# Expert slots by pairs in a two-layer mixture-of-experts kernel

## The chip, the cores and the metric

The kernel runs on one core of one Trainium2 chip. The time is the device time of one execution in microseconds (us); lower is better. TensorE (PE) multiplies, VectorE (DVE) and ScalarE (ACT) work on vectors, GpSimd (POOL) issues the indirect gathers and scatters, and SyncE (SP) issues the large transfers from HBM. Each engine runs its own program in order and waits on semaphores; branches are executed by every engine for itself.

## What is computed

Two blocks run one after the other. The first has two layers of attention and a mixture of experts, the second a mixer of three branches and a feed-forward part. The change is in the mixture of experts of the first block, which sees 512 tokens in layer 0 and 256 in layer 1:

```python
def hier_moe(h, w_group, b_group, w_router, b_router, w1, w3, w2):
    ...
    _, g_idx = lax.top_k(g_logits, 1)                      # one of 4 groups
    ...
    top_v, top_i = lax.top_k(e_in, TOP_K_IN_GROUP)         # two of its 8 experts
    weights = g_w * jax.nn.softmax(top_v, -1)
    experts = g_idx * EXPERTS_PER_GROUP + top_i
    ...
    def expert_block(a):
        xb, e = a
        return (jax.nn.silu(xb @ w1[e]) * (xb @ w3[e])) @ w2[e]
    ...
    return jnp.zeros((t, d), h.dtype).at[tok_s].add(w_s[:, None].astype(h.dtype) * yb[dest])
```

There are 32 experts a layer with 6 MB of weights each (w1 and w3 1024x512, w2 512x1024, all float32). How many rows an expert gets is known only on the chip.

## The kernel before

`route_tokens` works out on the chip which expert gets which rows. It counts the rows of every expert (`size`), ranks the experts by size, and gives each a column of a table of slots (`uc`), from which `gtab` (which rows to gather), the scatter tables and `meta`/`meta2` (expert number and count by place) are made. This is a chain of short DVE operations with a few small matmuls among them; the first gather (on POOL) waits for `gtab`, and PE for the gathered rows.

`experts` then has a fixed list of turns. The first two turns take the two largest experts ("any"). After them `round_(i)` stands nested, one for each i, with a place for a large expert (more than 64 rows; only as long as there can be one, `most[0]`, 15 in layer 0 and 7 in layer 1) and a place for a small one. Large experts fill their places from the front by size, small ones from the back, so the smallest come first. Each place is a branch on the count: `n > 0` runs the turn, the Else only transposes the rows for the next turn. The program stops at the first round in which both places are empty (L1185).

A turn (`turn`) loads six pieces of weights (`expert_weights`, L977 to L980; `wpiece` issues each on SP at L143, 1 MB, into a ring of 6 tiles plus 10 in layer 0 and 12 in layer 1), gathers the rows of the turn two turns ahead (`ahead`), and computes in blocks of up to 128 rows. By the number of rows a block is a quarter (up to 32, L1018 and L1035), a half (up to 64, L1046 and L1061) or full (L1071 and L1086). Each is a first group of matmuls over pieces 0 to 3 and a second over pieces 4 and 5. Between the two the rows of the next turn are transposed (`rows_T`, L995 on PE, L997 on ACT). ACT copies the result (`ys`, L1038, L1064, L1089), which is the end of a turn below, and POOL scatters it. A large expert with more than 128 rows goes on with `rest`; the branch around the rest (L1166) carries a hint for PE that it is likely taken.

SP runs ahead of PE as far as the ring lets it. Each transfer waits on the lane (semaphore) of the earlier transfer that used it, and on PE for the tile that it overwrites. In the Else of a place SP has no transfer to issue but raises the same semaphores by hand (L1180), each after the earlier transfer on that lane has landed, so that later waits count alike on both ways.

With this kernel's inputs layer 0 has 15 used experts and layer 1 has 14.

Of the kernel before, what the change touches and what calls it, by code (L numbers as in the profile page):

```python
# [19 lines left out]
P = 128  # L20
# [6 lines left out]
NE = 32  # L27
# [70 lines left out]
class Builder:  # L98
# [665 lines left out]
    def route_tokens(self, l, nt, gp, mp, rp):  # L764
# [11 lines left out]
        units = mt([NE, 2 * NE], "units")  # L776
        nc.vector.tensor_copy(units[:, 0:NE], self.iota[0:NE, 0:NE])
        nc.vector.tensor_scalar(units[:, NE:], self.iota[0:NE, 0:NE], -1.0, float(NE - 1), ALU.mult, ALU.add)
# [76 lines left out]
        rn = mt([NE, 2], "rn")  # L855
        nc.vector.tensor_reduce(rn[:, 0:1], before, AX.X, ALU.add)
        used = mt([NE, NE], "used")
        nc.vector.tensor_scalar(used, srow, 0.0, None, ALU.is_gt)
        nc.vector.tensor_reduce(rn[:, 1:2], used, AX.X, ALU.add)
# [5 lines left out]
        uh = mt([NE, 2 * NE], "uh")  # L865
        nc.vector.tensor_scalar(uh, units, uc, None, ALU.is_equal)
# [7 lines left out]
        nc.tensor.matmul(mb[0:NE, 0:2 * NE], lhsT=eix, rhs=uh, start=True, stop=True)  # L874
        mb2 = self.bankB()
        nc.tensor.matmul(mb2[0:NE, 0:2 * NE], lhsT=cnt, rhs=uh, start=True, stop=True)

        meta = keep([1, 4 * NE], "meta", I32)
        nc.vector.tensor_copy(meta[:, 0:2 * NE], mb[0:1, 0:2 * NE])
        nc.vector.tensor_copy(meta[:, 2 * NE:4 * NE], mb2[0:1, 0:2 * NE])  # L880
# [38 lines left out]
        for out, parts in ((tb, self.iota[:, 0:P]), (sb, self.cst[:, C_IOTAM:C_IOTAM + P]),  # L919
# [13 lines left out]
            if out is tb:  # L933
# [6 lines left out]
                meta2 = keep([1, 7 * NE], "meta2", I32)  # L940
                for i in range(2):
                    c = slice(2 * NE * i, 2 * NE * i + 2 * NE)
                    nc.vector.scalar_tensor_tensor(meta2[:, c], gtab[0:1, 0:2 * NE], 0.0, meta[:, c], ALU.mult, ALU.add)
# [3 lines left out]
                nc.vector.tensor_tensor(meta2[:, 6 * NE:7 * NE - 2], meta2[:, 4 * NE + 2:5 * NE],  # L947
                                        meta2[:, 5 * NE:6 * NE - 2], ALU.add)
# [33 lines left out]
    def experts(self, l, nt, mp, first, meta, meta2, gtab, stabs, XG, XE, ybuf):  # L982
# [121 lines left out]
        turns = [("any", 0, 0), ("any", 1, 1)]  # L1104
        for i in range(NE - 2):
            turns += [("large", i, 2 + i)] * (i < most[0]) + [("small", i, NE - 1 - i)]

        def ahead(k):
            if k + AHEAD < len(turns):
                kind, _, slot = turns[k + AHEAD]  # L1110
                gather(slot * nt, XG[k % AHEAD], 64 if kind == "small" else P)

        def turn(k, n, W):

            kind, i, slot = turns[k]
            x = XT[k % 2]
            groups = nt if kind == "any" else 1 + sum(i < m for m in most[1:nt]) if kind == "large" else 1

            def block(g, size, b=lambda: None):
# [4 lines left out]
                two(slot * nt + g, W, ht)  # L1124
# [625 lines left out]
```

## Time and profile before

| | us |
|---|---|
| median of 3 runs | 2325.39 (2325.28 to 2330.71) |
| profiled execution | 2326.15, its span 2324.3 |
| PE busy | 1948.4 (84%) |
| DVE, ACT, POOL busy | 1002.8 (43%), 739.9 (32%), 272.6 (12%) |
| HBM read | 455.65 MB, 202 GB/s over the span |

The span is the time from the first instruction to the last in one profiled execution. The granted clock of PE was 0.912 of full speed over it. The largest transfers are the expert weights, 174 pieces of 1 MB. The two mixture-of-experts stretches lie at about 415 to 800 us and 1055 to 1337 us.

To read the rows below: a row of a timeline gives the start, the duration, the engine, the line, the operation with what it writes and reads, the count of merged instructions, and in brackets how long the engine sat idle before it and what ended that. A row of a source line gives the number of instructions and their shortest, median and longest duration in ns, with the first and last start.

### The profile page before, as it was taken

How to read it: one execution, taken by the hardware profiler on the slowest of the kernel's cores; microseconds unless marked ns; L12 is line 12 of the kernel's file. 1: busy time of each engine (PE TensorE's matmuls, PEld its weight loads, DVE VectorE, ACT ScalarE, POOL GpSimd, SP SyncE). 2: the span in 40 equal slices, each digit the busy share in tenths (PEclk: the TensorE clock that was granted, in tenths of full speed). 3: DMA queues.
4: the chain of work that ended last, by engine and by line, in shares of the span. 5: the costliest groups of instructions: out<-in, count | busy, mean ns of one | idle time of the engine just before them, and what ended most of it. 6: DMA issues, size and time to landing. Idle time of an engine off the chain costs nothing. (4 is left out here: it accounts for less than half of the span.)

```text
span 2324.3 us, 27711 instructions
## 1 busy us (share of the span) xinstructions
PE 1948.4 (84%) x10138; PEld 1348.4 (58%) x10138; DVE 1002.8 (43%) x1956; ACT 739.9 (32%) x1322; POOL 272.6 (12%) x214
## 2 busy tenths in 40 slices
PE   6999796778876489977865549999899899998997
PEld 3656575334433167753432237777688677776885
DVE  3346655300000174561000056656654567566554
ACT  2233431100111154411111045444444355434442
POOL 0002301101111052120111102000200020002000
PEclk9999797789997789978987769999999999998998
DMA  9974115354767762156668764344455434454550
GB/s 396 375 280 155 65 37 217 130 209 187 317 255 296 276 239 70 42 205 273 242 253 340 307 241 169 129 145 168 163 186 185 152 129 147 143 181 150 184 181 29
DMA packets 75147, 456.01 MB, mean 196 GB/s; under 512 B 13544, under 2 KB 14092, under 8 KB 24496
## 3 DMA queue, kind: packets, MB, share of 16 engines
q1 hardware_dynamic: 61632, 430.99, 49.5%
q0 software_dynamic: 9664, 14.79, 1.8%
q10 hardware_dynamic: 3632, 7.37, 0.9%
q8 instruction: 129, 2.11, 0.4%
q14 instruction: 90, 0.74, 0.1%
HBM read 455.65 MB, written 13.30 MB: 202 GB/s over the span
## 5 line engine op out<-in xcount | busy, mean ns | idle before, releaser
L167 DVE TENSOR_TENSOR whl<-w,whl 128x1024 fp32r<-128x1024 f32 x312 | 397.1, 1287 | 234.9 <-ACT whl L166 224.2
L166 ACT ACTIVATE whl<-w 128x1024 fp32r<-128x1024 f32 x332 | 344.4, 1057 | 260.5 <-PE bankA L180 208.0
L178 PE MATMUL bankA<-whl,x2h 128*128 128x512 f32 (+1 forms) x864 | 345.3, 400 | 9.6 <-ACT x2h L238 7.2
L180 PE MATMUL bankA<-whl,x2l 128*128 128x512 f32 (+1 forms) x864 | 345.0, 400 | 5.8 <-DVE x2l L239 5.8
L179 PE MATMUL bankA<-whl,x2h 128*128 128x512 f32 (+1 forms) x864 | 342.0, 397 | 0.0
L178 PEld LDWEIGHTS bankA<-whl,x2h 128*128 128x128 f32 x864 | 168.4, 195 | 43.8 <-ACT x2h L238 8.2
L180 PEld LDWEIGHTS bankA<-whl,x2l 128*128 128x128 f32 x864 | 167.4, 194 | 40.6 <-DVE x2l L239 7.2
L179 PEld LDWEIGHTS bankA<-whl,x2h 128*128 128x128 f32 x864 | 167.9, 194 | 35.0 <-issue 2.0
L1071 PE MATMUL bankA<-w,xt 128*128 128x512 f32 x320 | 153.1, 641 | 17.2 <-issue 14.7
L1018 PE MATMUL bankA<-w,xt 128*32 128x256 f32 x1216 | 97.3, 463 | 55.5 <-DMA w<-in_wmoe 32.2
L178 PE MATMUL bankA<-whl,xh 128*128 128x512 f32 (+1 forms) x336 | 132.5, 395 | 5.4 <-ACT xh L238 5.4
L179 PE MATMUL bankA<-whl,xh 128*128 128x512 f32 (+1 forms) x336 | 129.4, 385 | 5.1 <-DVE whl L167 5.1
L180 PE MATMUL bankA<-whl,xl 128*128 128x512 f32 (+1 forms) x336 | 127.8, 384 | 0.1
L414 ACT ACTIVATE p<-bankS,sm 128x256 f32<-128x256 f32 (+2 forms) x160 | 85.7, 537 | 117.6 <-DVE sm L405 59.4
L1071 PEld LDWEIGHTS bankA<-w,xt 128*128 128x128 f32 x320 | 65.0, 206 | 99.7 <-issue 98.3
L213 POOL TENSOR_TENSOR sm<-sm,mhalf 128x1 f32<-128x1 f32 (+3 forms) x32 | 32.2, 1006 | 690.9 <-DVE sm L211 679.3
L1018 PEld LDWEIGHTS bankA<-w,xt 128*32 128x32 f32 x1216 | 47.7, 131 | 102.7 <-issue 44.7
L1022 DVE TENSOR_TENSOR s<-s,bankA 64x256 f32<-64x256 f32 x19 | 8.0, 423 | 221.9 <-ACT s L1021 221.9
L1000 POOL DMA_INDIRECT ybuf<-ys,stab x34 | 34.6, 1019 | 523.6 <-ACT ys L1038 147.1
L1075 DVE TENSOR_TENSOR s<-s,bankA 128x512 f32<-128x512 f32 x10 | 6.9, 688 | 195.2 <-PE bankA L1071 181.7
L178 PEld LDWEIGHTS bankA<-whl,xh 128*128 128x128 f32 x336 | 64.2, 191 | 32.0 <-ACT xh L238 7.4
L995 PE MATMUL bankB<-cst,xg 128*128 128x128 f32 (+1 forms) x328 | 40.4, 271 | 49.8 <-issue 31.6
(456 smaller groups left out, 2982.2 us busy)
## 6 DMA issues: line engine op xcount, KB each, us to landing
w<-in_wmoe SPq DMA_DIRECT2D x174, 1024.0 KB, 12.4
w<-in_wd SPq DMA_DIRECT2D x166, 1024.0 KB, 5.1
w<-in_wmod SPq DMA_DIRECT2D x48, 1024.0 KB, 7.5
y<-ybuf SPq DMA_DIRECT2D x12, 512.0 KB, 7.7
w<-in_rows SPq DMA_DIRECT2D x5, 1024.0 KB, 4.7
w<-mrow SPq DMA_DIRECT2D x7, 512.0 KB, 8.7
fbuf<-w SPq DMA_DIRECT2D x4, 512.0 KB, 2.8
nb<-in_nabias POOLq DMA_DIRECT2D x16, 128.0 KB, 2.5
```

The costliest lines, as they stand in the source:

```text
L166: nc.scalar.activation(h, s, AF.Copy)
L167: self.low = (eng or nc.vector).tensor_tensor(lo, s, h, ALU.subtract).ins
L178: mm(out, lhsT=xh, rhs=wh, start=start, stop=False)
L179: mm(out, lhsT=xh, rhs=wl, start=False, stop=False)
L180: mm(out, lhsT=xl, rhs=wh, start=False, stop=stop)
L213: self.power = self.nc.gpsimd.tensor_tensor(r, t, self.mhalf[:, :n], ALU.pow).ins
L414: nc.scalar.activation(p[:, :n], s[i][:, :n], AF.Exp, bias=nm[:, i:i + 1], accum_out=ss[:, i:i + 1])
L995: nc.tensor.transpose(xb[:, k], xg[0:rows, (4 * i + k) * P:(4 * i + k + 1) * P], self.ident[0:rows, 0:rows])
L1000: nc.gpsimd.indirect_dma_start(out=ybuf.rearrange("r (m d) -> (r m) d", m=1 << parts), out_offset=bass.IndirectOffsetOnAxis(ap=stabs[parts ...
L1018: nc.tensor.matmul(acc[r:r + 32], lhsT=xT[:, k, 0:32], rhs=wslice(W, m, k, 256 * f, 256), start=k == 0, stop=k == KT - 1)
L1022: nc.vector.tensor_tensor(s, s, acc[64:128], ALU.mult)
L1071: nc.tensor.matmul(acc[m], lhsT=xT[:, k], rhs=wslice(W, m, k), start=k == 0, stop=k == KT - 1)
```

## The change

In the routing the two tables of columns (from the front and from the back) become one. From its rank r, the number u of used experts and the number b of large ones (the two first included), an expert's place is worked out so that places 2 and 3, 4 and 5, ... are pairs: a large one and the smallest small one still left, as long as there are large ones, and then two small ones. That takes more operations on [32,1] columns. `meta` and `meta2` shrink.

In `experts` the list of turns and `round_` go. `pair(i)` has one branch on the first count. With fewer than 65 rows the Then runs two small turns, otherwise the Else runs a large turn and a small one. The second of each pair (`second`) can be empty and keeps an Else. The next pair is entered only if its first count is above 0. The branch of the pair gets a hint for PE, set in the pair before.

```diff
-        rn = mt([NE, 2], "rn")
-        nc.vector.tensor_reduce(rn[:, 0:1], before, AX.X, ALU.add)
...
-        few = mt([NE, 1], "few")
+        r, u, b, s, few, near, uc, t = (mt([NE, 1], f"slot{i}") for i in range(8))
+        nc.vector.tensor_reduce(r, before, AX.X, ALU.add)
+        for c, n in ((0.0, u), (64.0, b)):
+            over = mt([NE, NE], "over")
+            nc.vector.tensor_scalar(over, srow, c, None, ALU.is_gt)
+            nc.vector.tensor_reduce(n, over, AX.X, ALU.add)
         nc.vector.tensor_scalar(few, size, 64.0, None, ALU.is_le)
-        nc.vector.tensor_scalar(rn[:, 1:2], rn[:, 1:2], -1.0, float(NE), ALU.mult, ALU.add)
-        uc = mt([NE, 1], "uc")
-        nc.vector.scalar_tensor_tensor(uc, few, rn[:, 1:2], rn[:, 0:1], ALU.mult, ALU.add)
...
+        nc.vector.tensor_tensor(s, u, r, ALU.subtract)
+        nc.vector.tensor_tensor(t, s, b, ALU.subtract)
+        nc.vector.tensor_scalar(near, t, -1.0, None, ALU.is_lt)
...
+        nc.vector.scalar_tensor_tensor(uc, t, few, uc, ALU.mult, ALU.add)
...
-                for i, op in enumerate((ALU.is_gt, ALU.is_le)):
-                    v = meta2[:, (2 + i) * NE:(3 + i) * NE]
-                    nc.vector.scalar_tensor_tensor(meta2[:, (4 + i) * NE:(5 + i) * NE], v, 64.0, v, op, ALU.mult)
...
+                nc.vector.scalar_tensor_tensor(meta2, gtab[0:1, 0:2 * NE], 0.0, meta, ALU.mult, ALU.add)
...
-        def round_(i):
-
-            for k in [k for k, t in enumerate(turns) if k > 1 and t[1] == i]:
-                kind, _, slot = turns[k]
-                ahead(k)
-                at, e = (4 * NE + slot, slot) if kind == "large" else (5 * NE + i, NE + i)
-                n = load(meta2, at, T)
-                with tc.If(n > 0) as some:
-                    turn(k, n, self.expert_weights(wm, load(meta2, e, NE - 1, engines=[ENG.SP])))
-                with some.Else():
-                    next_rows(k)
-            if i + 1 < NE - 2:
-                with tc.If(load(meta2, 6 * NE + i + 1, 2 * T) > 0):
-                    round_(i + 1)
+        def second(k):
+
+            ahead(k)
+            n = load(meta2, NE + k, T)
+            with tc.If(n > 0) as some:
+                turn(k, "small", n, weights(k))
+            with some.Else():
+                next_rows(k)
+
+        def pair(i):
+
+            k = 2 + 2 * i
+            ahead(k)
+            n = load(meta2, NE + k, T)
+            if i < most[0]:
+                with tc.If(n < 65, label=f"pair{l}_{i}") as fewer:
+                    turn(k, "small", n, weights(k))
+                    second(k + 1)
+                with fewer.Else():
+                    turn(k, "large", n, weights(k))
+                    if i + 1 < most[0]:
+                        tc.mark_branch_hint_location(f"pair{l}_{i + 1}", "LikelyTaken", [ENG.PE])
+                    second(k + 1)
+            else:
+                turn(k, "small", n, weights(k))
+                second(k + 1)
+            if k + 2 < NE:
+                with tc.If(load(meta2, NE + k + 2, T) > 0):
+                    pair(i + 1)
 
         for k in range(2):
             ahead(k)
-            turn(k, load(meta, 2 * NE + k, T), first[k])
...
+            if k == 1:
+                tc.mark_branch_hint_location(f"pair{l}_0", "LikelyTaken", [ENG.PE])
+            turn(k, "any", load(meta, NE + k, T), first[k])
```

The program order of SP before, from the last piece of a small expert in layer 0 to the next branch of a place over the Else of its place (DMA are the pieces; DMAHW2 to DMAHW7 are the lanes; `meta` holds the counts):

```order
L143 DMA w<-in_wmoe 128x2048 [waits DMAHW7_49]
L1155 COMPARE_AND_BRANCH
L1155 UNCONDITIONAL_BRANCH x2
L1180 UNCONDITIONAL_BRANCH [waits SP_sequencer_49,DMAHW2_49,DMAHW3_49,DMAHW4_49,DMAHW5_49,DMAHW6_49,DMAHW7_49]
L1094 TENSOR_LOAD meta_3280
L1185 COMPARE_AND_BRANCH
L1094 TENSOR_LOAD meta_3280
L1180 COMPARE_AND_BRANCH
L1150 UNCONDITIONAL_BRANCH
```

In it the L1180 with six lanes is what SP runs where the place is empty. After, inside the Then of a pair in layer 0, from the fifth piece of its first expert over the branch of the second (L1181) to that one's first two pieces:

```order
L143 DMA w<-in_wmoe 128x2048 [waits DMAHW0_49]
L143 ISA
L143 DMA w<-in_wmoe 128x2048
L1160 COMPARE_AND_BRANCH
L1160 UNCONDITIONAL_BRANCH x2
L1096 TENSOR_LOAD meta_3295
L1181 COMPARE_AND_BRANCH
L1096 TENSOR_LOAD meta_3295
L143 ISA
L143 DMA w<-in_wmoe 128x2048 [waits DMAHW2_49]
L143 ISA
L143 DMA w<-in_wmoe 128x2048
```

Nothing that waits for all lanes stands between the two any more. And the head of the same Then, from the branch that enters the pair (L1192) over the first three pieces of its first expert:

```order
L1192 COMPARE_AND_BRANCH
L1096 TENSOR_LOAD meta_3295
L143 ISA
L143 DMA w<-in_wmoe 128x2048 [waits DMAHW4_49,DMAHW7_49,DMAHW3_49,PE_49]
L143 ISA
L143 DMA w<-in_wmoe 128x2048 [waits DMAHW5_49,DMAHW1_49,PE_49]
L143 ISA
L143 DMA w<-in_wmoe 128x2048 [waits DMAHW6_49]
```

The first two pieces of a pair's first expert wait on PE besides their lanes; the other pieces and all of the second expert's wait on lanes only.

The program order of PE before, from the end of the second turn to the first place of layer 0 (rows in the order of the program, not of execution; `xg` are the gathered rows):

```order
L1086 MATMUL bankA<-w,ht_0_3379 128x512 x8
L1144 UNCONDITIONAL_BRANCH x3
L1166 UNCONDITIONAL_BRANCH
L1094 TENSOR_LOAD meta_3280
L1191 COMPARE_AND_BRANCH
L1094 TENSOR_LOAD meta_3280
L1180 COMPARE_AND_BRANCH
L1746 BRANCH_PREFETCH_HINT
L995 MATMUL bankB<-cst,xg_0_3072 128x64
```

and after, the branch L1192 that enters the first pair, with the start of its Then, and further down the end of that Then and the head of its Else:

```order
L1096 TENSOR_LOAD meta_3295
L1212 COMPARE_AND_BRANCH
L1096 TENSOR_LOAD meta_3295
L1192 COMPARE_AND_BRANCH
L1160 COMPARE_AND_BRANCH
L1020 MATMUL bankA<-w,xt_0_3388 32x256 x32
L997 MATMUL bankB<-cst,xg_0_3069 128x64 x8
```

The turn of a large expert is not here any more. The end of that Then and the head of the Else behind it:

```order
L1063 MATMUL bankA<-w,ht_0_3391 64x512 x8
L1160 UNCONDITIONAL_BRANCH
L997 MATMUL bankB<-cst,xg_0_3068 128x128 x8
L1181 UNCONDITIONAL_BRANCH
L1767 BRANCH_PREFETCH_HINT x2
L997 MATMUL bankB<-cst,xg_0_3069 128x64
L1155 UNCONDITIONAL_BRANCH
L997 MATMUL bankB<-cst,xg_0_3069 128x64 x7
L1073 MATMUL bankA<-w,xt_0_3388 128x512 x16
L1081 MATMUL bankB<-cst,s 128x128 x4
```

The large turn, which followed the branch of its place at once, now stands behind the two small turns of the Then; the two hints at the head of the Else belong to the branch of the next pair and to the branch around the rest.

## Rows read from the trace of the kernel before

**Rows 1.** Timeline of ACT: ends of turns in layer 0 and layer 1.
```profile
691.23 0.39 ACT L1038 ACTIVATE ys<-bankA 128x256 f32<-128x256 f32 x1 [1.91 <-PE bankA L1035]
...
794.03 0.60 ACT L1064 ACTIVATE ys<-bankA 128x512 f32<-128x512 f32 x1 [4.31 <-PE bankA L1061]
...
1147.83 0.38 ACT L1038 ACTIVATE ys<-bankA 128x256 f32<-128x256 f32 x1 [1.91 <-PE bankA L1035]
...
1276.72 0.38 ACT L1038 ACTIVATE ys<-bankA 128x256 f32<-128x256 f32 x1 [2.51 <-PE bankA L1035]
...
1293.15 0.38 ACT L1038 ACTIVATE ys<-bankA 128x256 f32<-128x256 f32 x1 [2.60 <-PE bankA L1035]
...
1309.69 0.38 ACT L1038 ACTIVATE ys<-bankA 128x256 f32<-128x256 f32 x1 [2.51 <-PE bankA L1035]
...
1330.20 0.60 ACT L1064 ACTIVATE ys<-bankA 128x512 f32<-128x512 f32 x1 [4.97 <-PE bankA L1061]
```

**Rows 2.** Stretches: us, busy times by engine, granted clock, DMA share, GB/s.
```profile
508.00:515.00 7.00, 6.03 (x17) 2.97 (x18) 0.03 (x1) 0.66 (x2) 3.04 (x3) 0.76 0.94 321
680.00:795.00 115.00, 73.25 (x591) 34.00 (x589) 5.78 (x13) 16.16 (x35) 17.06 (x18) 0.81 0.77 289
...
1256.00:1316.00 60.00, 31.80 (x330) 14.29 (x332) 2.14 (x6) 5.31 (x15) 8.83 (x9) 0.77 1.00 397
```

**Rows 3.** Waits of SP, 680 to 800 us: total us, times, longest.
```profile
SPq L1180 <- SPq L1180: 56.5, 23, 4.5
```

**Rows 4.** Source line L143: from issue to landing of its transfers.
```profile
DMA to landing us min/median/max: 4.7/6.8/17.8
```

**Rows 5.** Timeline of PE: turns and their waits, in both layers.
```profile
571.50 1.11 PE L995 MATMUL bankB<-cst,xg 64*128 64x64 f32 x8 [3.62 <-DMA xg<-fbuf,gtab]
...
780.87 7.08 PE L1046 MATMUL bankA<-w,xt 128*64 128x512 f32 x30 [1.50 <-DMA w<-in_wmoe]
...
1274.72 1.93 PE L1035 MATMUL bankA<-w,ht 128*32 128x256 f32 x32 [0.38 <-DVE ht L1028]
...
1313.37 10.69 PE L1046 MATMUL bankA<-w,xt 128*64 128x512 f32 x32 [3.75 <-issue]
```

**Rows 6.** PE's branches, ns: L1180 in three stretches, then five skipped rests (L1166).
```profile
L1180 PEldq COMPARE_BRANCH  x1: 6282/6282/6282, 691.1 to 691.1; - x1
...
L1180 PEldq COMPARE_BRANCH  x3: 77/6290/6523, 708.9 to 726.1; - x3
...
L1180 PEldq COMPARE_BRANCH  x8: 65/200/437, 1200.2 to 1257.0; - x8
...
L1166 PEldq COMPARE_BRANCH  x1: 3462/3462/3462, 500.3 to 500.3; - x1
...
L1166 PEldq COMPARE_BRANCH  x1: 358/358/358, 675.5 to 675.5; - x1
...
L1166 PEldq COMPARE_BRANCH  x1: 5711/5711/5711, 1068.5 to 1068.5; - x1
...
L1166 PEldq COMPARE_BRANCH  x1: 359/359/359, 1097.2 to 1097.2; - x1
...
L1166 PEldq COMPARE_BRANCH  x1: 2235/2235/2235, 1166.1 to 1166.1; - x1
```

**Rows 7.** Timeline of DVE in the routing of layer 0.
```profile
399.37 0.17 DVE L858 TENSOR_SCALAR used<-bankB 32x32 f32<-32x32 f32 x1
...
399.96 0.62 DVE L864 SCALAR_TENSOR_TENSOR uc<-few,rn 32x1 f32<-32x1 f32 x1
400.61 0.24 DVE L866 TENSOR_SCALAR uh<-units,uc 32x64 f32<-32x64 f32 x1
```

**Rows 8.** End of layer 0: PE's last branches (ns), and SP's first y loads.
```profile
L1185 PEldq COMPARE_BRANCH  x2: 2857/3147/3437, 791.0 to 794.9; - x2
...
800.14 0.81 SPq L1202 DMA_DIRECT2D y<-ybuf  x2
```

More of the change, by code (lines that the diff above doesn't have):

```diff
@@ L774, in keep @@
             return mp.tile(shape, dt, name=f"{name}{l}")
-        units = mt([NE, 2 * NE], "units")
-        nc.vector.tensor_copy(units[:, 0:NE], self.iota[0:NE, 0:NE])
-        nc.vector.tensor_scalar(units[:, NE:], self.iota[0:NE, 0:NE], -1.0, float(NE - 1), ALU.mult, ALU.add)
         lift = mt([P, 2, NE], "lift")
@@ L1103, in experts, with next_rows, turn @@
         most = [(2 * T - 2) // (n + 1) for n in (64, 128, 256, 384)]
-        turns = [("any", 0, 0), ("any", 1, 1)]
-        for i in range(NE - 2):
-            turns += [("large", i, 2 + i)] * (i < most[0]) + [("small", i, NE - 1 - i)]
+        sized = lambda k: "any" if k < 2 else "small" if k % 2 or (k - 2) // 2 >= most[0] else "large"
         def ahead(k):
[L1109 to L1115, printed above, removed]
+            if k + AHEAD < NE:
+                gather((k + AHEAD) * nt, XG[k % AHEAD], 64 if sized(k + AHEAD) == "small" else P)
+        def next_rows(k):
+            if k + 1 < NE:
+                rows_T(XG[(k + 1) % AHEAD], XT[(k + 1) % 2], 64 if sized(k + 1) == "small" else P)
+        def turn(k, kind, n, W):
+            i = (k - 2) // 2
             x = XT[k % 2]
             groups = nt if kind == "any" else 1 + sum(i < m for m in most[1:nt]) if kind == "large" else 1
+            m = meta2 if k > 1 else meta
             def block(g, size, b=lambda: None):
@@ L1123, in block @@
                 one(W, x, ht, b)
-                two(slot * nt + g, W, ht)
+                two(k * nt + g, W, ht)
             def rest(g):
@@ L1130, in rest @@
                 if more:
-                    with tc.If(load(meta2 if k > 1 else meta, 2 * NE + slot, T, engines=[ENG.Pool]) > P * (g + 1)):
-                        gather(slot * nt + g + 1, XE)
+                    with tc.If(load(m, NE + k, T, engines=[ENG.Pool]) > P * (g + 1)):
+                        gather(k * nt + g + 1, XE)
                 if g > 1:
@@ L1149, in turn @@
                 tc.mark_branch_hint_location(label, "LikelyTaken", [ENG.PE])
-                with tc.If(load(meta2 if k > 1 else meta, 2 * NE + slot, T, engines=[ENG.Pool]) > P):
-                    gather(slot * nt + 1, XE)
+                with tc.If(load(m, NE + k, T, engines=[ENG.Pool]) > P):
+                    gather(k * nt + 1, XE)
             if kind == "large":
@@ L1167, in turn, with weights @@
                     rest(1)
[L1169 to L1186 removed]
+        def weights(k):
+            return self.expert_weights(wm, load(meta2, k, NE - 1, engines=[ENG.SP]))
@@ L1188, in experts @@
         for k in range(2):
             ahead(k)
-            turn(k, load(meta, 2 * NE + k, T), first[k])
-        with tc.If(load(meta2, 6 * NE, 2 * T) > 0):
-            round_(0)
+            if k == 1:
+                tc.mark_branch_hint_location(f"pair{l}_0", "LikelyTaken", [ENG.PE])
+            turn(k, "any", load(meta, NE + k, T), first[k])
+        with tc.If(load(meta2, NE + 2, T) > 0):
+            pair(0)
     def combine(self, l, ybuf, rw, nt, ahead, tp):
```

35 lines of the change are left out of this document (16 added, 19 removed).

## The prediction

> **What bounds the kernel now.** The span has two mixture-of-experts stretches, about 415 to 800 us (layer 0) and 1055 to 1337 us (layer 1), and the change touches nothing else. I went from the end times of turns on ACT to what held them. In layer 0 the turn of the three-row expert, the last one before an empty place, ends at 691.23 and the last turn at 794.03: 102.8 us for five small experts [rows 1]. In layer 1 the turn that ends at 1147.83 is followed by 182.4 us to the last end at 1330.20; where nothing empty stands between (1276.72, 1293.15, 1309.69) a small expert takes 16.43 and 16.54 us [rows 1]. Six pieces of weights come in a turn, so a piece takes **2.75 us**. The stretch 1256 to 1316 shows why: the DMA engines are busy all of the time there (share 1.00, 397 GB/s), while 680 to 795 has 0.77 and 289 [rows 2]. What empties the queue there is SP: at an empty place it takes the Else of L1180 and waits, lane by lane, until the earlier weights have landed; 56.5 us in 23 waits between 680 and 800 [rows 3]. So the tails are bound by weight transfer, and the empty places put holes into it. The rest of both stretches (large experts) is bound by PE.
>
> With the inputs given, layer 0 routes to 15 experts (165 and 118 rows in the two first turns, large 216, 139, 138, 80, small 58, 53, 29, 18, 4, 3, 1, 1, 1) and layer 1 to 14 (61, 79; 133, 119; 56, 24, 12, 9, 8, 6, 2, 1, 1, 1). Ten places are empty before; one after (the last of layer 0). Layer 0 becomes (216,1) (139,1) (138,1) (80,3) (4,18) (29,53) (58,empty), layer 1 (133,1) (119,1) (1,2) (6,8) (9,12) (24,56).
>
> **The tail of layer 0.** In the new order of SP's program the second expert of a pair waits on lanes alone, but the first one of a pair waits on PE before its first two pieces: for the first piece until the preceding turn's first matmuls are done, for the second until that turn has ended. So the queue still stops once in each pair. A piece issued into an empty queue lands 4.7 us later at best [rows 4]. First expert: 4.7 + 4 x 2.75, and 1.2 from the last piece to the end (half of L1035's 1.93 us and a copy [rows 5]) = 16.9; second: 16.5. Pair (4,18): 33.4. Pair (29,53): PE arrives 6 us late at 29, over a jump that I cost below, which leaves about 17.3 instead of 16.9; 53 is a half turn: its fourth piece lands 11.0 after 29's last (9.8 after 29's data-bound end), then the last quarter of L1046 (2.7, from 10.69 for all [rows 5]) and 6.1 from the end of L1046 (780.87 + 7.08) to the copy at 794.03 [rows 1, 5], about 18. For 58: 0.6 of register loads, a jump of 6.3, L1046 of about 9 (7.08 and 10.69 at the two clocks [rows 5]) and 6.1 = 22.0. Sum 33.4 + 17.3 + 18 + 22 = 90.7 against 102.8: **12.1 saved** (8 to 20: 20 with a piece at 2.5, 8 with L1046 at its longest and a second jump).
>
> **The tail of layer 1.** The ring is larger here, and only expert 6 (both pieces) and expert 9 (as above) wait on PE. Counted from 1147.83: 119's second piece lands at +4.7, sixteen more at 2.75 bring the last of expert (1) at +48.7, its end at +49.9. Expert 2: 16.5. Expert 6: first piece only at 2's end, 4.7 + 5 x 2.75 + 1.2 = 19.7. Expert 8: 16.5; 9: 16.9; 12: 16.5; 24: 17.3 (a jump again); 56: 20.5 as now (1309.69 to 1330.20 [rows 1]; its PE work, with 3.75 of a jump and 10.69 of L1046 [rows 5], is longer than its transfer). Sum 173.8 against 182.4: **8.6 saved** (5 to 15).
>
> The Trainium skill speaks against such a stream: "DMA: Bandwidth & Descriptors", section "Where 436 GB/s comes from", says that for transfers out of HBM a core is bound at about 358 GB/s. By that a piece would take 2.93 us (an estimate), and the two sums, with some 65 pieces on the path, would be 12 us longer. The trace disagrees: 397 GB/s over 60 us [rows 2].
>
> **What it adds: jumps on PE.** A pair now starts with one branch, L1192. Its Then (two small turns, for a pair without a large expert) stands first, and every pair with a large expert jumps over it: 419 instructions on PE (matmul and weight load counted each). The trace has the price of jumps. Over 317 instructions, the empty large places before: 6.28, and 6.29 to 6.52 in the next two; the short ones over 78 instructions in layer 1: at most 0.44 [rows 6]. None of the long ones was hinted. The change marks the pair branch with a hint, and before has hinted jumps too, the skipped rests (235 or 388 instructions): 0.36 twice, 2.23, 3.46, 5.71 [rows 6]. In the built program the hint of the first pair of each layer is missing; the four others are there, each as the first of two hints at the head of the Else. So:
> - 216 and 133, no hint: 6.3 each. The DMA engines are at 0.94 when 216 starts [rows 2], so a fetch of code shares the queue as it did at 691. 12.6.
> - 139: hidden up to the 3.62 us in which its first transpose waits for its gathered rows [rows 5]; 0.
> - 138 and 80: hinted. I take 2.2, the middle of the five: 4.4. If the 5.71 is right for them: 11.4, and 2.1 for 139.
> - 119: PE may lose some 4 us and still be earlier than the transfer of expert (1); 0.
> Together **17.0 lost** (2, if jumps were near ones, to 26).
>
> At the end of a pair of two small ones PE jumps over the Else of that pair (389 to 631 instructions), also 6.3; the first two pieces of the next pair have landed by then, the fourth only at 10.2, so it costs a quarter turn under 1 us and only the half turn 58 all of it; both are in the sums above. With large experts the smaller lead of the ring costs nothing that I can find: the second piece lands 4.7 after the small turn's end, and PE wants it only after the first fourth of the large turn's first matmuls, some 5 us after that end.
>
> **What it adds: routing.** Between the row comparison and the column of slots DVE has 17 small operations for 5 before. 5 took from 399.37 to 400.61 with one of 0.62 among them [rows 7]; a dependent one follows the one ahead after 0.10 to 0.20, so 12 more are 2.0 us a layer, and the gather tables and with them the first gather come later by as much: **4.0 lost** (2.4 to 6). The meta2 operations that go away come after the gather table; nobody waits for them; 0. Nor do the two `units` operations lie on the path; 0.
>
> **What it adds: the end of layer 0.** The second place of (58,empty) is empty. PE jumps over its body, transposes once more, jumps over the pair's Else and only then reaches the last branch. At that end DMA is quiet and a jump took 3.44 and 2.86 [rows 8]. SP starts the y loads when the last scatter has landed, at 800.14 [rows 8], and after the change also waits for PE's last event, by two such jumps some 8 us after the last turn's end; 800.14 is 6.1 after it. **2 lost** (0 to 5).
>
> **The sum.** 12.1 + 8.6 - 17.0 - 4.0 - 2.0 = -2.3: the profiled execution of 2326.15 us would become 2328.4. The median of the runs is 0.8 below that execution, so 2327.7, rounded **2328 us**: no difference that a measurement of this kernel can tell (about 0.3%, 7 us).
>
> **Rivals.**
> - *Cheap jumps* (faster). Long jumps cost what near or well-hinted ones do, 0.36 each: 2.2 instead of 17.0, and the time is 2326.15 + 12.5 lower = 2313.7, 2313 against the median. For it: two hinted jumps at 0.36. Against: three unhinted ones of 317 in a row at 6.3, and two branches without a hint. With a piece at 2.5 us besides, 2300.
> - *Dear hints* (slower). The hint does not hold over two turns of code; 138 and 80 pay 5.7 and 139 2.1: 26.1 lost, 2337.5, 2337 against the median. For it: 5.71 with a hint, and that hint was the second of its block. Against: it is the rest's hint that stands second now. From 1.0 us per hinted jump on the change is slower than before, from 4.2 by more than 0.3%.
>  The Trainium skill sides with this rival: "Runtime: NRT & Kernel Launch", section "Instruction fetch mechanics", says that a taken branch to code outside the current two pages of 256 instructions has to fetch it first. By that all six pair jumps would pay, and the time would be about this rival's. The trace agrees for the 317s and disagrees for the hinted 235s at 0.36.
> - *Each pair drains* (slower). If the pair's merge holds SP as the Else of L1180 does now, the first of a pair takes about 20 us instead of 16.9, as 6 does in my sum: some 3.4 for each of five pairs, 12 with what the half turns hide of it: 2340. For it: lanes are still waited for in that order. Against: the Else that waits is executed once.
> - *The empties stay*: ranks of equal sizes would have to collide; the comparison that orders them is unchanged. 0.02.
>
> **How the numbers follow.** Forecast 0.50 (2319 to 2332), cheap jumps 0.20, dear hints 0.18, drained pairs 0.10, rest 0.02. Faster by over 0.3% 0.20 (under 2318.4), within 0.50, slower 0.30. The range leaves out a tenth on either side: 2311 to 2340.
>
> **What would show it.** Right: idle time of PE of about 6 us ahead of the first matmul of 216 and of 133, and a few us or less ahead of 138 and 80; no long SP wait between 700 and 780; the first-to-last end of the small turns about 91 us in layer 0 and, from the one-row turn between 133 and 119, about 174 us in layer 1; the gap from the routing's row comparison to the first gather 2 us longer. Wrong: a PE that starts 216 without a pause, a DMA share under 0.85 in the tails, or small turns above 20 us.

## The result: slower by 0.8%

Over ten runs each the changed kernel took 2345.16 us (2331.91 to 2354.18) and the kernel before 2325.76 us (2315.27 to 2330.71): a ratio of 1.008, 95% interval 1.0055 to 1.0104. The forecast was 2328 with a range up to 2340; the time lies outside of it. The profiled execution of after took 2354.18, which is 9.0 above its own median, so the sums below, made between two profiled executions (+28.0), are larger than the difference of the medians (+19.4).

ACT's ends of turns answer [rows 1]. They are timeline rows: start, duration, engine, line, operation, and in brackets the idle time before and what ended it.

```profile
546.16 0.60 ACT L1091 ACTIVATE ys<-bankA 128x512 f32<-128x512 f32 x1 [16.60 <-PE bankA L1088]
...
714.92 0.38 ACT L1040 ACTIVATE ys<-bankA 128x256 f32<-128x256 f32 x1 [1.94 <-PE bankA L1037]
734.22 0.38 ACT L1040 ACTIVATE ys<-bankA 128x256 f32<-128x256 f32 x1 [2.66 <-PE bankA L1037]
749.23 0.38 ACT L1040 ACTIVATE ys<-bankA 128x256 f32<-128x256 f32 x1 [2.61 <-PE bankA L1037]
768.62 0.38 ACT L1040 ACTIVATE ys<-bankA 128x256 f32<-128x256 f32 x1 [2.66 <-PE bankA L1037]
788.74 0.60 ACT L1066 ACTIVATE ys<-bankA 128x512 f32<-128x512 f32 x1 [4.36 <-PE bankA L1063]
812.90 0.60 ACT L1066 ACTIVATE ys<-bankA 128x512 f32<-128x512 f32 x1 [5.06 <-PE bankA L1063]
...
1182.77 0.38 ACT L1040 ACTIVATE ys<-bankA 128x256 f32<-128x256 f32 x1 [1.97 <-PE bankA L1037]
...
1358.23 0.60 ACT L1066 ACTIVATE ys<-bankA 128x512 f32<-128x512 f32 x1 [4.36 <-PE bankA L1063]
```

The tail of layer 0 is 714.92 to 812.90, 98.0 us against 102.8; that of layer 1 1182.77 to 1358.23, 175.5 against 182.4. Both are shorter. All the same the last turn ends 28.0 later. From differences of such ends, stage by stage:

| stretch (end of turn to end of turn) | before | after | predicted | found |
|---|---|---|---|---|
| start to the 118-row turn (with routing of layer 0) | 506.53 | 507.99 | +2.0 | +1.5 |
| 118 rows to (3): four large pairs, layer 0 | 184.70 | 206.93 | +10.7 | **+22.2** |
| tail of layer 0 | 102.80 | 97.98 | -12.1 | **-4.8** |
| last turn of layer 0 to the 61-row turn (end of layer 0, attention, routing) | 277.90 | 283.15 | +4.0 | +5.3 |
| 79-row turn | 31.51 | 35.30 | 0 | +3.8 |
| 133 rows and its small turn | 44.39 | 51.42 | +6.3 | +7.0 |
| tail of layer 1, with 119 rows in it | 182.37 | 175.46 | -8.6 | -6.9 |
| sum | | | +2.3 | +28.0 |

What SP waits for between 705 and 820 answers [rows 3] (total us, times, longest):

```profile
SPq L143 <- DMA w<-in_wmoe: 37.9, 9, 14.3
SPq L143 <- PE bankB L997: 18.4, 3, 9.4
SPq L1181 <- SPq L1181: 8.4, 2, 5.4
```

The 23 waits of 56.5 us at L1180 are gone; SP now waits at the issue of a piece, for an earlier piece or for PE. The 8.4 us at L1181 belong to the one empty place that is left. The stretches show the stream (us, busy times by engine, granted clock, DMA share, GB/s), as [rows 2]:

```profile
715.00:813.00 98.00, 59.29 (x441) 23.57 (x442) 4.37 (x10) 8.51 (x21) 10.06 (x10) 0.81 0.84 329
...
1280.00:1340.00 60.00, 32.66 (x359) 16.27 (x357) 2.86 (x8) 6.23 (x16) 7.47 (x8) 0.77 0.99 391
```

The loss is on PE, at the head of each large turn: the rows of its timeline that answer 571.50 of [rows 5], and the pair branch L1192 (in ns: shortest, median, longest) that answers [rows 6].

```profile
518.02 1.09 PE L997 MATMUL bankB<-cst,xg 64*128 64x64 f32 x8 [9.25 <-issue]
519.03 16.76 PE L1073 MATMUL bankA<-w,xt 128*128 128x512 f32 x32
...
538.13 8.80 PE L1088 MATMUL bankA<-w,ht 128*128 128x512 f32 x16 [0.83 <-issue]
...
585.97 1.08 PE L997 MATMUL bankB<-cst,xg 64*128 64x64 f32 x8 [5.80 <-issue]
586.99 15.21 PE L1073 MATMUL bankA<-w,xt 128*128 128x512 f32 x32
...
633.06 0.68 PE L997 MATMUL bankB<-cst,xg 64*128 64x64 f32 x8 [4.18 <-issue]
633.68 15.70 PE L1073 MATMUL bankA<-w,xt 128*128 128x512 f32 x32
```

```profile
L1192 PEldq COMPARE_BRANCH  x4: 3947/4764/7563, 510.0 to 675.7; - x4
...
L1192 PEldq COMPARE_BRANCH  x2: 6523/6668/6812, 1133.3 to 1182.6; - x2
```

Each of the six large turns pays its jump of 419 instructions, hinted or not: 7.56 (no hint), 5.51, 4.02, 3.95, then 6.81 (no hint) and 6.52. The first group of matmuls behind the idle stretch is slower too, 16.76, 15.21 and 15.70 us where it takes 14.00 in a kernel without the jump (below). Not all of that is new: three rows of the kernel before, at 216, 139 and 80, show it slow at the first two already.

```profile
509.58 15.70 PE L1071 MATMUL bankA<-w,xt 128*128 128x512 f32 x32
...
572.55 16.71 PE L1071 MATMUL bankA<-w,xt 128*128 128x512 f32 x32
...
659.18 14.00 PE L1071 MATMUL bankA<-w,xt 128*128 128x512 f32 x32
```

### The profile page after: what moved, and what is told of

Its sections match the earlier page's. It is cut to its first block, busy times and chain, and to the rows that moved or that the text cites. A ratio compares the mean times of both kernels' runs of the same rounds, so it can differ in the third digit from the quotient of the medians.

```text
span 2352.4 us, 27189 instructions
## 1 busy us (share of the span) xinstructions
PE 1946.6 (83%) x10066; PEld 1346.2 (57%) x10066; DVE 1005.5 (43%) x1968; ACT 733.3 (31%) x1304; POOL 264.0 (11%) x205
## 5 line engine op out<-in xcount | busy, mean ns | idle before, releaser
L1073 PE MATMUL bankA<-w,xt 128*128 128x512 f32 x320 | 158.4, 658 | 17.2 <-issue 14.8
L1073 PEld LDWEIGHTS bankA<-w,xt 128*128 128x128 f32 x320 | 67.1, 213 | 103.1 <-issue 101.7
L1088 PE MATMUL bankA<-w,ht 128*128 128x512 f32 x160 | 73.0, 610 | 7.9 <-DVE ht L1082 6.3
## 6 DMA issues: line engine op xcount, KB each, us to landing
w<-in_wmoe SPq DMA_DIRECT2D x174, 1024.0 KB, 14.1
y<-ybuf SPq DMA_DIRECT2D x12, 512.0 KB, 10.3
```

The costliest lines, as they stand in the source:

```text
L1073: nc.tensor.matmul(acc[m], lhsT=xT[:, k], rhs=wslice(W, m, k), start=k == 0, stop=k == KT - 1)
L1088: nc.tensor.matmul(yb[m], lhsT=hT[:, k], rhs=w2slice(W, k, m * 512, 512), start=k == 0, stop=k == 3)
```

## The experiments

Theory: the pair branch is what costs, by its far jumps and the lower clock behind them. Rivals: the hints are at fault; the ring of weight tiles is (both ways of the branch take tiles, only one uses them); or the order of the experts itself is worth little.

**Are hints worth anything?** Without those of the pair branch:

```diff
                     turn(k, "large", n, weights(k))
-                    if i + 1 < most[0]:
-                        tc.mark_branch_hint_location(f"pair{l}_{i + 1}", "LikelyTaken", [ENG.PE])
                     second(k + 1)
...
```

> The changed kernel without the hints on the pair branch; all else as in the change. Theory J (a jump of PE over the two small turns fetches its code anew, and a hint set two turns earlier saves a part of the fetch): the jumps to 139, 138, 80 and 119, 5.51, 4.02, 3.95 and 6.52 us with a hint, go to 6.3 to 7.6 like the two without one, idle time ahead of 138 and 80 from 4.2 to about 6.5, and the kernel is 4 to 8 us slower than the change (2349 to 2353). Rival N (the hint does nothing, the shorter jumps are chance): same as the change within 3 us, jumps of 4 to 7 as before.

Measured: 2344.28 (2342.83 to 2345.61), the same as after. Its jumps take 6.02, 5.40, 3.93, 4.09, 6.37 and 6.54. The hint of the pair branch, first of two in its block, bought nothing at any of its four places.

With that hint left alone in its block, the hint of the rest removed there:

```diff
             if groups > 1:
-                tc.mark_branch_hint_location(label, "LikelyTaken", [ENG.PE])
+                if kind == "any":
+                    tc.mark_branch_hint_location(label, "LikelyTaken", [ENG.PE])
```

> The changed kernel with the hint of the pair branch alone in a large turn; the hint on the branch around the rest, which stood second in the same block, is gone. Theory D (the second hint displaces the first): jumps to 139, 138, 80 and 119 fall to under 1 us, 9 to 14 us faster than the change (2331 to 2336). Theory J (one hint does not hold over two turns whatever stands beside it): the pair jumps stay at 4 to 6.5, and the skipped rest of 80 and 119 costs up to 6 more, mostly beside L1088: within 4 us of the change.

Measured: 2351.47 (2351.19 to 2356.97), no better. The hinted jumps take 3.56, 0.35 (138), 3.72 and 4.83; 0.35 alone lies far below what these jumps took without a hint or with one that did nothing. The skipped rest of 119, now without a hint, takes 6.05 where it took 0.38 in after (L1171 there, L1172 here):

```profile
L1171 PEldq COMPARE_BRANCH  x1: 375/375/375, 1208.4 to 1208.4; - x1
```

```profile
L1172 PEldq COMPARE_BRANCH  x1: 6047/6047/6047, 1202.2 to 1202.2; - x1
...
1210.41 2.78 PE L1020 MATMUL bankA<-w,xt 128*32 128x256 f32 x44 [1.09 <-DMA w<-in_wmoe]
```

That cost nothing: it ran beside 7.13 us of L1088's matmuls, and PE was idle for 1.09 behind them, as in after (1.07). What the heads gained went elsewhere. Between 500 and 720 us PE waited 15.7 us ahead of the first transposes of large turns instead of 23.4, and 6.8 ahead of small turns where after had no such wait (total us, times, longest):

```profile
PE bankB L997 <- issue: 15.7, 3, 8.1
PE bankA L1020 <- issue: 6.8, 2, 3.6
```

These two stand behind the rests of 139 and 138, where the short jump at L1149 took 3.32 and 2.95 us instead of 0.36 and 0.33; why it did isn't shown. So a hint can work, but it did nothing as the first of two in a block, and seldom all that it could: the rest of 80 took 4.72 with its hint and 4.83 without.

**What would pairs be worth without their branch?** The number of pairs with a large expert is written into the program, 4 and 2, so that this kernel holds for these inputs alone:

```diff
-            if i < most[0]:
-                with tc.If(n < 65, label=f"pair{l}_{i}") as fewer:
...
-            else:
-                turn(k, "small", n, weights(k))
-                second(k + 1)
+            turn(k, "large" if i < (4, 2)[l] else "small", n, weights(k))
+            second(k + 1)
...
```

> The pair branch is gone: the first four pairs of layer 0 and two of layer 1 are written as a large and a small turn, the others as two small ones, which fits these inputs alone. Routing, pairs and the end are the change's. Theory J: PE goes from the small turn to the next large one in about 1.5 us, as before, the 31 us between the two traces' large turns (layer 0: 507 to 691, layer 1: 1103 to 1148) fall to under 6, and with the tiles of one branch not taken the first small expert of a pair waits no more on PE, 18.8 to 19.4 us to about 16.5: 2306 to 2316. Rival T (the loss is in routing, gathers or the clock, and the jump hides behind weights that come late anyway): at most 10 us faster than the change, 2335 or more.

Measured: 2255.88 (2254.38 to 2259.17), ratio 0.9723 [0.9698, 0.9748]. That is 2.8% under before and some 50 us beyond what I had expected of it: the branch costs not the 17 us of the sum but about 89 (2345.16 to 2255.88; 83 by the two ratios to the kernel before). Two of the ends show a part that no jump explains:

```profile
682.21 0.38 ACT L1040 ACTIVATE ys<-bankA 128x256 f32<-128x256 f32 x1 [1.94 <-PE bankA L1037]
693.03 0.38 ACT L1040 ACTIVATE ys<-bankA 128x256 f32<-128x256 f32 x1 [2.69 <-PE bankA L1037]
701.52 0.38 ACT L1040 ACTIVATE ys<-bankA 128x256 f32<-128x256 f32 x1 [1.96 <-PE bankA L1037]
```

The turns of (4) and (18) take 10.8 and 8.5 us, less than six pieces at 2.75: part of their weights were there already, loaded during the large turn. In after they take 19.3 and 15.0. The next two runs show that this is mostly the ring.

**The ring apart from the jumps.** First the fixed pairs with twelve tiles per pair taken and not used, as the way not taken does in after:

```diff
             second(k + 1)
+            if i < most[0]:
+                for _ in range(12):
+                    self.wtile()
```

> The fixed pairs, without pair branch or jump, but with twelve further tiles taken from the ring after each pair and never used, as the way not run takes them in the change. Theory R: small turns in the tails back to about 95 us in layer 0 and 170 in layer 1, large turns as in the fixed pairs: 2256 + 45 to 50 = 2301 to 2306. Rival J: within 15 us of the fixed pairs, at most 2271.

Measured: 2287.83 (2284.61 to 2290.87), 32 us more than with the whole ring (23 by the ratios) and less than the 45 to 50 that the theory had. The profiles have it in the tails: 81.4 and 169.4 us against 73.4 and 148.4 in the fixed pairs; the stretches of large turns are the same within 0.5. Then the other way round, the changed kernel with the pair's tiles taken ahead of its branch, the same for both ways:

```diff
             if i < most[0]:
+                one, two = ([self.wtile() for _ in range(6)] for _ in range(2))
                 with tc.If(n < 65, label=f"pair{l}_{i}") as fewer:
-                    turn(k, "small", n, weights(k))
-                    second(k + 1)
+                    turn(k, "small", n, weights(k, one))
+                    second(k + 1, two)
...
```

> The change with one set of twelve tiles for a pair, taken ahead of its branch and filled by whichever way runs; the branch with its jumps, routing and order are the change's. Theory R (both ways of the branch take tiles of the ring, so half of the ring is passed over and the first small expert of a pair can't be loaded during the large turn ahead of it; that costs the tails some 50 us): the small turns behind the last large one as in the fixed pairs, 73 us instead of 98 in layer 0 and 148 instead of 175 in layer 1, the idle times ahead of the large turns as in the change: 2290 to 2300. Rival J (nearly all of the 89 us between the change and the fixed pairs comes from jumps and the clock behind them): no more than 20 us faster than the change, 2325 or more.

Measured: 2326.17 (2321.46 to 2329.08), ratio 0.9998 [0.9976, 1.0019]: 19 us better than after, and level with before. The ring shortened both tails, to 82.7 and 160.6 us from 98.0 and 175.5 ((4) and (18) take 9.5 and 11.3), but less than expected, and four jumps became dearer (last section). So the 89 us are made of both: with the ring lost the branch costs 57 (after against e7), with the ring whole 70 (e5 against e3).

The kernel with the lost ring and no branch shows what the heads of the large turns would be. PE's timeline at 216 and 139, to be held against the rows of after above:

```profile
511.23 0.68 PE L997 MATMUL bankB<-cst,xg 64*128 64x64 f32 x8 [1.05 <-DVEq L1171]
511.84 14.00 PE L1073 MATMUL bankA<-w,xt 128*128 128x512 f32 x32
...
570.15 0.71 PE L997 MATMUL bankB<-cst,xg 64*128 64x64 f32 x8
570.79 2.84 PE L1073 MATMUL bankA<-w,xt 128*128 128x512 f32 x6
```

Most of the 57 lies there. The six large turns of after are 13.1, 6.6, 5.9, 6.6, 9.8 and 5.8 us longer than these, 48 in all (38.17 for 25.11 us at 216, and so on); their jumps are 34.4 of it, the rest is mostly the slower matmuls. In the tail of layer 0 after is 16.5 us longer, 10.3 of it at (58) behind the jump at the end of a pair. And 139 starts here without the 3.62 us wait for its rows.

The granted clock says why they are slower. Stretches of the first groups at 216 and 139 in after, and at 216 without the jump (the clock is the third number from the end):

```profile
519.00:536.00 17.00, 16.79 (x33) 7.08 (x32) 0.10 (x1) 1.14 (x3) 0.94 (x1) 0.83 0.93 383
587.00:602.00 15.00, 15.00 (x33) 6.48 (x32) 0.00 (x0) 1.09 (x3) 0.94 (x1) 0.92 1.02 418
```

```profile
512.00:526.00 14.00, 13.84 (x32) 5.84 (x32) 0.05 (x1) 1.01 (x3) 3.66 (x4) 1.00 0.64 239
```

After 9.25 and 5.80 us of idle PE, the clock is 0.83 and 0.92 of 2.4 GHz, so part of the group ran at 1.2; in this kernel, without the idle stretch, it is 1.00. An idle stretch right ahead isn't the only way to the lower clock: before had only 1.67 us of idle PE ahead of 216, and its group took the 15.70 us shown above.

**Another way around the branch: share the small second.** The pair's weights are loaded ahead of the branch, the branch holds the first turn alone, and one small second turn stands behind it:

```diff
+            W = weights(k)
             if i < most[0]:
...
+                with tc.If(n > 64) as big:
+                    turn(k, "large", n, W)
+                with big.Else():
+                    turn(k, "small", n, W)
...
+            second(k + 1)
...
```

> The weights of a pair's first expert are issued ahead of the branch, the large turn stands first and is entered without a jump, the small one is its Else, and the second turn stands once behind both. PE jumps 203 instructions at the end of a large turn (beside its last matmuls) and 318 at the head of a pair of small ones (beside the transfer of its weights). Theory J: both are hidden, the ring holds as many experts ahead as before, 2310 to 2320. Rival L (each jump of over 200 costs its 4 to 6 us wherever it stands): 2330 to 2340.

Measured: 2302.06 (2292.29 to 2305.44), ratio 0.9905 [0.9871, 0.9939]. The head is free now, but at the end of the large turn PE jumps 203 instructions over the small one and waits 2.9 to 5.4 us ahead of the small turns behind it (three in this row, another 5.25 at 700.39; PE's waits, 500 to 700: us in total, times, longest):

```profile
PE bankA L1020 <- issue: 12.4, 4, 5.4
```

**Is it the order of the two ways?** The changed kernel with the large way first, so that large pairs are entered without a jump and jump over 515 instructions at their end:

```diff
-                with tc.If(n < 65, label=f"pair{l}_{i}") as fewer:
-                    turn(k, "small", n, weights(k))
+                with tc.If(n > 64) as many:
+                    turn(k, "large", n, weights(k))
                     second(k + 1)
-                with fewer.Else():
-                    turn(k, "large", n, weights(k))
+                with many.Else():
+                    turn(k, "small", n, weights(k))
                     second(k + 1)
...
```

> The changed kernel with the two ways of the pair's branch exchanged: the large turn and its small one stand first, the two small turns behind them, and the pair branch has no hint. Large pairs are entered without a jump and jump over some 515 instructions at their end; small pairs jump over some 530 at their head. Theory one (a jump costs where PE has nothing queued): the jump at the end of a large pair stands behind only the last matmuls of a small turn and is exposed like the one at the head, so the six large turns keep 4 to 6 us each of the seven to eight they lost: 2330 to 2348, no gain over the changed kernel. Rival (it is the place of the jump that matters): ahead of the large turns nothing is paid, and the jump behind is hidden by some 2 us of matmuls and costs 2 to 4: 2312 to 2328. A time under 2300 would mean that the order of the two ways alone is the whole loss.

Measured: 2349.07 (2343.8 to 2353.06), ratio 1.0111 [1.0084, 1.0138]; no gain. 216 is free (27.4 us instead of 38.2), but at the end of its pair stands a jump of 5.67 us:

```profile
L1160 PEldq COMPARE_BRANCH  x1: 5671/5671/5671, 569.2 to 569.2; - x1
```

and PE's timeline shows 139 waiting behind it as it did in after:

```profile
576.41 1.09 PE L997 MATMUL bankB<-cst,xg 64*128 64x64 f32 x8 [5.72 <-issue]
```

**No pair branch at all.** One turn for both kinds, which picks quarter, half or full block as the two first turns do:

```diff
-            if kind == "large":
-                block(0, 0, lambda: next_rows(k))
-            else:
+            if True:
                 with tc.If(n < 33) as fewer:
...
+            turn(k, "large" if i < most[0] else "small", n, weights(k))
+            second(k + 1)
...
```

> The pair branch is gone for any input: the first turn of a pair picks quarter, half or full block inside the turn, as the first two turns of a layer do, and has one set of tiles; the second turn stands once behind it. A large turn jumps over the quarter and the half (122 and 78 instructions), a small one skips half, full and rest. Theory R with J: ring as in the fixed pairs, two short jumps for each large turn at 0.3 to 0.5 and now and then 3 to 6, six of them: 2265 to 2290. Rival L (each skipped body costs a fetch): above 2300.

Measured: 2299.49 (2298.69 to 2300.91), ratio 0.9879 [0.9836, 0.9922]. The ring is whole, but this is no better than the rival's 2300: a large turn still jumps over the smaller blocks at its head, with PE idle (here 139):

```profile
577.39 16.55 PE L1073 MATMUL bankA<-w,xt 128*128 128x512 f32 x32 [5.01 <-issue]
```

Then, from that kernel, with the full block first in all turns that have one (`few` holds the choice between quarter and half):

```diff
+                with tc.If(n > 64) as many:
+                    block(0, 0, lambda: next_rows(k))
+                with many.Else():
+                    few()
...
```

> As e6_one_turn_for_both (no branch of the pair; its first turn picks quarter, half or full block by the number of rows), but the full block stands first in the program and the choice between quarter and half behind it, in the two first turns of each layer as well. So large blocks are entered without a jump and small ones over a jump of about 200 instructions; at a full block's end PE has to jump over the small ones instead. Theory one (what a jump costs is set by what PE could have done meanwhile): e6 paid 4.5 to 4.8 us of jump ahead of 139, 138, 80 and 119 with an idle PE; these go, and the jump at the end of a full block falls behind matmuls already queued and costs 1 us or less; the four large turns and the two second turns of the layers come to within 2 us of those of e3_fixed_pairs; the small first turns of pairs gain a jump that a wait for weights hides. Time 2262 to 2278. Rival: the jump at the end of the full block is exposed as that behind the merge of e4_shared_second was (2 to 4 us a turn), and what is saved ahead is paid behind: 2290 to 2302, no difference from e6_one_turn_for_both (2299.5). Second rival: the small turns, now over a jump each, take 3 to 5 us more in the tails: 2280 to 2295.

Measured: **2257.8** (2251.18 to 2258.46), ratio 0.9699 [0.9678, 0.9719], for any input: 67 us under before, and level with the fixed pairs. The jump at the end of 139's full block is no cheaper; the branch's row (ns):

```profile
L1166 PEldq COMPARE_BRANCH  x1: 5880/5880/5880, 576.9 to 576.9; - x1
```

But its 5.88 us begin with the 7.13 us of L1088's matmuls and are over ahead of their end. In PE's timeline the next matmul waits for nothing:

```profile
576.85 7.13 PE L1088 MATMUL bankA<-w,ht 128*128 128x512 f32 x16 [0.78 <-DVE ht L1082]
583.82 1.04 PE L997 MATMUL bankB<-cst,xe 128*128 128x128 f32 x8
```

How much of this the kernel before could have had without pairs, by the order of blocks in its two first turns alone:

```diff
+                    with tc.If(n > 64) as many:
+                        block(0, 0, lambda: next_rows(k))
+                    with many.Else():
+                        few()
...
```

> The kernel before with one edit: in the two first turns of each layer the full block stands first in the program, and the choice between quarter and half behind it. Separates what e8_full_block_first gained by the order of its blocks from what it gained by pairs. Theory (a far jump was already paid by the kernel before at its second turns): the idle time of 8.00 and 6.70 us ahead of the first matmuls of those turns falls to some 2, the matmuls behind it take 14 instead of 16, and the turn of 118 rows takes 24 instead of 32.5, that of 79 rows 24.5 instead of 31.5: 15 to 16 us saved, 2308 to 2312, ratio 0.993 to 0.994; the pairs themselves are then worth some 50 of e8's 67 us. Rival: the rows or weights of the next turns are late by as much, and the gain is given back there: 2318 to 2326.

Measured: 2315.42 (2310.26 to 2319.83), ratio 0.9961 [0.9944, 0.9978], half of what was expected. The second turns gain as foreseen (8.6 and 7.9 us), but the 61-row turn, a half block, now stands two blocks down. Its jump over the full block took 0.39, but the next one, over the quarter (121 instructions, 0.38 before), 6.12:

```profile
L1156 PEldq COMPARE_BRANCH  x1: 6116/6116/6116, 1050.4 to 1050.4; - x1
```

In the timeline PE is idle for 5.47 of it:

```profile
1056.78 5.54 PE L1046 MATMUL bankA<-w,xt 128*64 128x512 f32 x18 [5.47 <-issue]
```

So of the 67 us some 8 come from the order of the blocks there, and some 58 (2315.42 to 2257.8) from pairs with a whole ring whose jumps lie behind matmuls; up to 5.5 of these 58 are the wait at 61 rows, which the kernel of 2257.8 does not have.

## Where the prediction was right and where it failed

**Jumps at the large turns: the term that failed.** The sum had 17.0 for the six. In the two stretches of large turns the profile has +22.2 and +7.0, 29.2. For 138 and 80 I took 2.2 from hinted jumps; 4.02 and 3.95 came, and e1 shows that the hints there did nothing. *Dear hints* had the nearest price (26.1 lost: 12.6 at the two without a hint, 2.1 at 139 and 5.7 twice); its reason, the distance alone, doesn't fit the 0.35 of e2 over the same two turns. "Runtime: NRT & Kernel Launch", section "Instruction fetch mechanics" of the Trainium skill, has a rule that the code of a far branch must be fetched first. All six of 3.95 to 7.56 agree with it.

What no case of mine had was what the jumps cost besides their duration. At 216 it is +10.7 instead of 6.3: PE was idle 7.6 us longer than before (9.25 for 1.67), and the matmuls behind took 3.1 longer, in the main the first group, 16.76 for 15.70, and L1088's, 8.80 for 7.11. At 138 and 80 it is +5.1 and +5.9: 3.4 and 3.5 of idle time, and the rest slower matmuls, whose first groups took 15.70 and 15.93 for 14.00.

For 139 the argument held against before, in part by luck: +0.7 for a jump of 5.51. The idle time grew by 2.2, from the wait of 3.62 to 5.80, but the first group took 15.21 where before took 16.71. And the wait is not there in the new order without the branch, so what was called hidden was a gain that the jump ate. For 119 it held: (1) ended 49.5 after the end at 1182.77, 49.9 was forecast.

**"With large experts the smaller lead of the ring costs nothing that I can find": wrong.** I looked at PE's need within the large turn alone, and there it held (e7 against e3 above). The lead is worth most later: weights loaded during large turns are the start of the tail, and a ring in which the other way's tiles stay empty holds fewer of them. 19 us with the branch (e5), 32 without (e7 against e3). This isn't part of what the sum missed, since its tails were priced with the stops at each pair; it is what the change gave away.

**The tail of layer 0: 4.8 saved instead of 12.1.** Both the pieces and what the first of a pair does with them I had wrong. The timeline of PE at (4) and (29):

```profile
717.41 0.62 PE L1020 MATMUL bankA<-w,xt 128*32 128x256 f32 x4 [2.54 <-DMA w<-in_wmoe]
724.23 6.19 PE L1020 MATMUL bankA<-w,xt 128*32 128x256 f32 x60 [6.20 <-DMA w<-in_wmoe]
...
754.15 1.07 PE L1020 MATMUL bankA<-w,xt 128*32 128x256 f32 x4 [4.99 <-issue]
758.89 5.93 PE L1020 MATMUL bankA<-w,xt 128*32 128x256 f32 x60 [3.67 <-DMA w<-in_wmoe]
```

I ended such a turn 1.2 us after its last piece. In fact 60 of its 64 first matmuls wait for the third piece. At (4) that landed 9.3 us after the end of the turn ahead, where the sum had 4.7 + 2.75 = 7.5. The 60 then take 6.19 at the clock left by the wait (3.66 for all 64 at full clock in e8); with what follows that is 10 us of PE's own work, more than the pieces still to come need. So (4) took 19.3 for 16.9, (29) 19.4 for 17.3. The half turns took 20.1 for 18 and 24.2 for 22, the last over a jump at the pair's end:

```profile
795.66 1.94 PE L1048 MATMUL bankA<-w,xt 128*64 128x512 f32 x2 [7.01 <-issue]
```

(18) was quicker, 15.0 for 16.5. *Each pair drains* fell as a mechanism: no wait for all lanes stands between pairs; but its 20 us for the first of a pair came close. The size of these holes was wrong, not their place. Two of the prediction's signs of being wrong did show here, if barely: a DMA share of 0.84 (715 to 813), under 0.85, and small turns above 20 us.

**Right:** the tail of layer 1 (175.5 us, forecast 173.8), though there too the first turns of pairs, 6, 9 and 24, took 1.0 to 1.9 more than forecast and expert 2 made up for it with 14.1 for 16.5; the transfer rate in it (391 GB/s beside 397 of [rows 2]); the routing, in which DVE's first and last step around the slots are now

```profile
400.22 0.15 DVE L848 COPY size<-bankB 32x1 f32<-32x1 f32 x1 [0.46 <-PE bankB L846]
...
404.88 0.27 DVE L879 TENSOR_SCALAR ua<-cst,slot 32x128 f32<-32x128 f32 x1
```

4.66 us apart for 2.50 before, +2.2 where 2.0 was put. From the last turn of layer 0 to the first of layer 1 it was +5.3. The larger part is the end of layer 0: SP's first y load stands 9.8 us after the last turn's end, where it stood 6.1 after it [rows 1, 8]. That is +3.7 where 2 was forecast.

```profile
822.66 0.81 SPq L1223 DMA_DIRECT2D y<-ybuf  x2
```

The first stretch of the table, +1.5 for +2.0, is near by luck. The routing's step at 400.22 came 1.9 us later than before, which is scatter (396.4 to 400.4 in the variants with the same code there), and what follows it took its 2.2; but the turn of 118 rows was 3.3 shorter, since a jump at its head took 3.11 instead of 6.27.

**Left out:** the 79-row turn, +3.8. Nothing in it was edited. Its head waits 9.90 us (L1073 at 1105.88) over two jumps of 2.76 and 2.99, where it waited 6.70 before, over jumps of 2.75 and 0.23. Why the second became dear isn't settled; in e9, with the full block first, the turn loses this wait.

## What to carry to other kernels

Price a far branch where PE has nothing queued, at what its jumps take there plus the slower matmuls after it, and take no hint at its word until a trace shows it; better, put the larger block first, so that the jump falls behind its matmuls, where a fully paid 5.9 us cost nothing. A branch whose two ways each take buffers from a ring takes them from both: pick the tiles ahead of it. And look at a change that costs little for what it stands in the way of: here the reordering itself was worth some 50 to 64 us (e9 to e8, and e3 against before), and its branch ate all of it.

## What the hardware showed besides

- A jump of the same 419 instructions took 3.93 to 7.62 us where no hint stood alone in its block (after, e1, e5, and the two without a hint in e2). With the stream of weights at 412 to 415 GB/s the four at 139, 138, 80 and 119 took 6.03 to 7.09 (e5); at 355 and 365 GB/s 138 and 80 took 4.02 and 3.95 (after); with a DMA share of 0.03 and 0.28 two far ones took 3.44 and 2.86 [rows 8]. Fetches of code that share the queue would do that, but 5.40 at 370 GB/s beside 3.93 at 381 (e1) shows that it isn't this alone. No run changed the traffic by itself.
- These two stretches are the jumps of 138 in after and in e5:

```profile
628.59:632.61 4.02, 0.29 (x8) 0.00 (x0) 0.00 (x0) 0.38 (x1) 2.24 (x3) 1.00 0.97 355
```

```profile
625.48:631.51 6.03, 0.28 (x8) 0.00 (x0) 0.00 (x0) 0.38 (x1) 3.05 (x3) 0.93 1.01 412
```

- Short jumps aren't always cheap: over 121 instructions one took 6.12 us (e9, at 61 rows) and one 0.38 (before, the same turn); the eight over 78 in layer 1 of before took at most 0.44 [rows 6]. The rule of the Trainium skill named above ("Runtime: NRT & Kernel Launch", section "Instruction fetch mechanics") lets such a jump be dear or cheap by where its target lies from what has been fetched; no run here shows the fetch itself.
